# Two routing tables of a mixture-of-experts kernel, made from kept 16-bit one-hots in a row of products instead of one 32-bit one-hot at a time

## The chip, the cores and the metric

The kernel runs on one core of a Trainium2 chip. The metric is the device time of one execution in microseconds (us). Three runs of the kernel before gave 2086.29, 2083.27 and 2085.58 us, so a median of 2085.58.

## The reference

A network of two layers works on 1024 tokens of width 1024. Each layer has a mixer (a gated convolution in layer 0, sliding-window attention in layer 1), a normalisation, a mixture of 32 experts, and a second normalisation. The experts, cut to what matters here:

```python
g_idx = argmax(g_logits)                       # one of 4 groups a token
top_p, top_i = top_k(softmax(e_sel), 2)        # two of the group's 8 experts
gates = g_p * top_p / sum(top_p)               # a gate for each (token, choice)
# the rows that chose an expert are put in blocks of 128 rows; a block runs through
# its expert, and each row of the result is scaled by its gate and added to its token
ys = (silu(x @ wg[e]) * (x @ wu[e])) @ wd[e]
out = segment_sum(ys * row_gate[:, None], row_tok)
```

An expert that more than 128 tokens chose needs further blocks, the overflow. All of it is in 32 bits.

## The kernel before, in words

Products are made on the tensor engine (PE) in three parts: each 32-bit operand is split into a high and a low part, and `mm3` issues high by high, high by low and low by high. Weights come in chunks of 1 MB from SyncE's DMA queue into rings of buffers. ScalarE (ACT) makes a chunk's high part (`h`, L164), VectorE (DVE) its low part (`l`, L165), and then the raw buffer is free for a later chunk. The kernel's instructions keep the written order on each engine (`manual_schedule`, L50).

`proj_route` (L398) routes the tokens, 128 at a time. `place` (L514) finds for a token and a choice its place in its expert's list (`pos`) and makes a one-hot of that place over 128 slots, in 16 bits (`oh`, L522), in a tile of two buffers that is dropped after `tabulate` (L526) has used it for the table of token numbers.

`experts` (L718) then goes through the 32 experts, one block of 128 rows each. For expert e the order on PE is: half of the gate product `pg`, the other half, half of the up product `pu`, the transposes of the next block's rows (`xpose`, L731), the other half of `pu`, then the down product of expert e-1 (`pd`), and the transposes of the hidden values (`hid_pose`, L767). Chunks are split three ahead. After each of the first three halves of an expert, `extra` (L777) takes one step of a generator that makes what the routing still lacks: the softmax gates (`gates`, L601), the table of gates by slot and expert (`slot_gates`, L625), which `y_out` first needs at the third expert, and the overflow's tables (`overflow`, L643), which are needed after the last expert. So there are three steps an expert, and they are spread over the first 13 experts.

`slot_gates` makes, for each of the 16 pairs of a token block and a choice, a 32-bit one-hot of the place (`goh`, L636) and a row of the gate at the chosen expert (`ga`, L637), both on GpSimd (POOL), and adds their 32-bit product on PE into one PSUM tile (`pgate`, L630). `overflow` makes for each pair a 32-bit one-hot (`ooh`, L694) and two rows (`orr`, L696) on VectorE, one pair a step, and PE adds their product to `pov` (L698) at the next step.

Two more places matter. `xsplit` (L738) puts the split rows of a block in the tiles xh and xl, but those of the first block in the slots `yt0` and `yt1`, in which `y_out` (L762) puts the experts' results from the third expert on; each slot has one buffer. A tile that takes over a slot is written only when the last reader of the tile before it is done.

Of the kernel before, what the change touches and what calls it, by code (L numbers as in the profile page):

```python
# [11 lines left out]
F32 = mybir.dt.float32  # L12
F32R = mybir.dt.float32r
F16 = mybir.dt.float16
I32 = mybir.dt.int32
AF = mybir.ActivationFunctionType
OP = mybir.AluOpType
AX = mybir.AxisListType

P = 128  # L20
D = 1024
T = 1024
NB = T // P
NE = 32
EG = 8
NG = 4
DE = 512
NOV = 16
ALPHA = 4 ** 0.25
# [6 lines left out]
def moe_net_kernel(ctx, tc, a, dbg=None):  # L36
# [15 lines left out]
    # ---------------------------------------------------------------- weights  # L52
    # a chunk is 1 MB; each partition reads one contiguous run of 8 KB, so that tile s of a chunk of n
    # tiles holds its rows n * p + s
# [42 lines left out]
    # The raw chunks lie in rings of two: two rings always, except that heads of q take the second during  # L97
    # the attention, a third from the output projection to the experts' last, and four chunks in the room of
    # the mixer's output, from when it has been read to the experts' last.
# [17 lines left out]
    def pump(eng=nc.sync):  # L117
        while st["load"] < min(len(chunks), st["limit"]):
            i = st["load"]
            r = rings[i]  # L120
            if st["free"][r] == 0:
                return
            st["free"][r] -= 1
            st["load"] += 1
            if r == "rawy":
                raws[i] = st["ry"][st["rawy"] % 4].rearrange("p k f -> p (k f)")
                st["rawy"] += 1
            else:
                p = st[r] if r in ("rawb", "rawx") else rawp
                raws[i] = p.tile([P, 2048], F32, name=f"raw{i}", tag=r, bufs=2)  # L130
            src = chunks[i][0]
            if i == 1:
                # the first two chunks come in alternate quarters, that the work may start
                for q in range(4):
                    for j in range(2):
                        x = chunks[j][0].rearrange("p k f -> p (k f)")[:, q * 512:(q + 1) * 512]
                        nc.sync.dma_start(raws[j][:, q * 512:(q + 1) * 512], x)
            elif i > 1:
                eng.dma_start(raws[i].rearrange("p (k f) -> p k f", k=src.shape[1]), src)
# [6 lines left out]
    # 32 KB in two halves: the mixers' output, chunks, the norm's rows, heads of q  # L146
# [49 lines left out]
    def warm(n, ps, tag, bufs):  # L196
        # products for nothing where the tensor engine waits, that its clock stays up
        t = ps.tile([P, 512], F32, name=f"warm{n}", tag=tag, bufs=bufs)
        for _ in range(n):
            nc.tensor.matmul(t.rearrange("p (k f) -> p k f", k=4), ones16,  # L200
                             ones16[:, None, :].to_broadcast([P, 4, P]), start=True, stop=True)
# [8 lines left out]
    # -------------------------------------------------------------- constants  # L210
# [54 lines left out]
    # ------------------------------------------------- bias rows of attention  # L265
# [3 lines left out]
    def bias_rows(w, ps):  # L269
        tab = w.tile([32, 16], F32, name="tab")  # L270
        nc.gpsimd.dma_start(tab, a["rel_table"])
        oh = w.tile([32, 384], F32, name="oh")
        nc.gpsimd.dma_start(oh, a["buckets"])
        far = w.tile([16, 384], F32, name="far")
        nc.gpsimd.memset(far, -BIG)
        yield
        pb = ps.tile([16, 384], F32, name="pb", tag="mm", bufs=8)
        nc.tensor.matmul(pb, tab, oh, start=True, stop=True)
        nc.vector.tensor_copy(far[:, P:2 * P], pb[:, P:2 * P])
        nc.gpsimd.dma_start(bias_v, far)  # L280
        # row q lies q further right, so that a plain rectangle of it holds the relative positions
        nc.gpsimd.dma_start(bass.AP(tensor=bias_s.tensor, offset=bias_s.offset, ap=[[8193, P], [512, 16], [1, 384]]),
                            bass.AP(tensor=bias_v.tensor, offset=bias_v.offset, ap=[[0, P], [384, 16], [1, 384]]))

    # ------------------------------------------------------------ layer 0: A
    def mixer_in(y):
        with ExitStack() as s:
# [19 lines left out]
            # v, tokens on partitions  # L307
# [26 lines left out]
            # u, channels on partitions  # L334
# [15 lines left out]
            # spatial mixing of v and y_a  # L350
# [12 lines left out]
            # gated convolution  # L363
# [33 lines left out]
    # ------------------------- B: projection, residual, norm, routing, tables  # L397
    def proj_route(l, y, c0, resid, bias, x1d, acc, R, xgs):  # L398
        s = R["stack"]
        with ExitStack() as s2:  # L400
# [113 lines left out]
            def place(n):  # L514
                t = w.tile([P, NE], F32, name=f"q{n}", tag="rq", bufs=2)
                oh = w.tile([P, 2, P], F16, name=f"oh{n}", tag="oh", bufs=2)
# [19 lines left out]
            if bias is not None:  # L536
                # the residual is scaled by ALPHA after its bias
                nc.vector.tensor_scalar(bias, bias, 1.0 / ALPHA, None, op0=OP.mult)
# [61 lines left out]
    # ------------------------------------------ gates and overflow bookkeeping  # L600
    def gates(w, R):  # L601
        lg, em, mx = R["lg"], R["em"], R["mx"]
        ge = w.tile([P, NB, NG], F32, name="ge")
# [8 lines left out]
        s = w.tile([P, NB, 4], F32, name="gs")  # L612
# [8 lines left out]
        # the sum that they enter is the residual's, over ALPHA  # L621
        nc.vector.scalar_tensor_tensor(s[:, :, 3:4], s[:, :, 2:3], 1.0 / ALPHA, s[:, :, 0:1], op0=OP.mult, op1=OP.mult)
        nc.vector.tensor_tensor(R["gate"], pr, s[:, :, 3:4].to_broadcast([P, NB, 2]), op=OP.mult)

    def slot_gates(w, ps, R):  # L625
        pt = ps.tile([P, 512], F32, name="pgate", tag="misc", bufs=1)
        made, used = [], 0
        for make, use in ((4, 0), (2, 0), (4, 4), (6, 6), (0, 0), (0, 6)):
            for i in range(used, used + use):
                nc.tensor.matmul(pt[:, 0:NE], *made[i], start=(i == 0), stop=(i == 15))  # L630
            used += use
            for i in range(len(made), len(made) + make):
                n, j = i // 2, i % 2
                oh = w.tile([P, P], F32, name=f"goh{i}", tag="goh", bufs=6)
                ag = w.tile([P, NE], F32, name=f"ga{i}", tag="ga", bufs=6)
                nc.gpsimd.tensor_scalar(oh, slots, R["pos"][:, n, j:j + 1], None, op0=OP.is_equal)  # L636
                nc.gpsimd.tensor_scalar(ag, R["A"][:, n, j], R["gate"][:, n, j:j + 1], None, op0=OP.mult)  # L637
                made.append((oh, ag))
            if used < 16:
                yield  # L640
        nc.vector.tensor_copy(R["sgate"], pt[:, 0:NE])

    def overflow(w, ps, R):  # L643
# [6 lines left out]
        ov = w.tile([P, NE], F32, name="ov")  # L650
# [14 lines left out]
        ovs = w.tile([P, NE], F32, name="ovs")  # L665
# [22 lines left out]
        nc.vector.scalar_tensor_tensor(slot, q, -float(P), pos, op0=OP.mult, op1=OP.add)  # L688
        po = ps.tile([P, 512], F32, name="pov", tag="misc", bufs=1)
        gate = R["gate"].rearrange("p n j -> p (n j)")  # L690
        for i in range(16):
            oh = w.tile([P, P], F32, name=f"ooh{i}", tag="goh", bufs=6)
            rr = w.tile([P, 2, 16], F32, name=f"orr{i}", tag="ga", bufs=6)
            nc.vector.tensor_scalar(oh, slots, slot[:, i:i + 1], None, op0=OP.is_equal)  # L694
            for j, x in enumerate((rowm[:, i // 2:i // 2 + 1], gate[:, i:i + 1])):
                nc.vector.tensor_scalar(rr[:, j], slots[:, 0:16], oid[:, i:i + 1], x, op0=OP.is_equal, op1=OP.mult)  # L696
            yield
            nc.tensor.matmul(po[:, 0:32], oh, rr.rearrange("p j b -> p (j b)"), start=(i == 0), stop=(i == 15))  # L698
        nc.vector.tensor_scalar(R["ovidx"], po[:, 0:16], float(T), None, op0=OP.add)
        nc.vector.tensor_copy(R["ovgate"], po[:, 16:32])  # L700
# [16 lines left out]
    # ------------------------------------------------------------ the experts  # L717
    def experts(l, c0, x1d, acc, R, xg, consts, scratch):  # L718
        with ExitStack() as s:
# [4 lines left out]
            # the block after the last expert's is the first of those for the rows beyond an expert's 128  # L724
# [13 lines left out]
            def xsplit(e):  # L738
                # the first block's lie where the results will, that the second's need not wait
# [251 lines left out]
    # ---------------------------------------------- norm of residual and experts  # L991
    class Norm2:
        # the parts of the norm of residual and experts, block by block
# [64 lines left out]
        def beside(self, block, fix, more, gate):  # L1058
            # the rows of the block are done again with what it adds
# [30 lines left out]
    # ------------------------------------------------------------ attention  # L1090
    def attention(qs, kh, kl, v):
        with ExitStack() as s:
# [10 lines left out]
            # a unit's four heads lie even ones first  # L1103
# [92 lines left out]
    # ================================================================ program  # L1196
    def routing_state(p, l):
# [6 lines left out]
            "idx": p.tile([P, NE], I32, name=f"idx{l}"), "sgate": p.tile([P, NE], F32, name=f"sgate{l}"),  # L1204
            "meta": p.tile([P, 17], I32, name=f"meta{l}"), "ovidx": p.tile([P, 16], I32, name=f"ovidx{l}"),
# [41 lines left out]
    with ExitStack() as s0:  # L1247
        kvp = pool("kv", st=s0)
        # a head's q, and k, each lie as the high part above the low one
# [157 lines left out]
def layout(inputs):  # L1407
# [9 lines left out]
    # channel tiles u, then (gate c, h, gate b) per tile, two tiles a chunk  # L1417
# [33 lines left out]
```

## Time and profile before

| what | value |
|---|---|
| median of 3 runs | 2085.58 us (2083.27 to 2086.29) |
| profiled execution, its span | 2086.2 us |
| PE busy | 1931.8 us (93%) |
| PE weight load busy | 1565.7 us (75%) |
| VectorE busy | 1580.8 us (76%) |
| ScalarE busy | 1206.1 us (58%) |
| GpSimd busy | 476.9 us (23%) |
| weight DMA queue (q1) | 487.41 MB, 61.6% of 16 engines' span |

The page gives no time of the profiled execution beside its span; the span lies 0.1 us under the slowest of the three runs, so that nothing to be seen lies around it. Busy time is the union of an engine's instructions. Matmuls are pipelined and their ends are modelled, so starts are the surer reading. A wait is named by what released it.

### The profile page before, as it was taken

To read this page: it belongs to the slowest core of one execution; us is meant where nothing else is said; L and a number is where in the kernel's file an instruction comes from. 1 tells how busy PE (TensorE), PEld (TensorE's weight loads), DVE (VectorE), ACT (ScalarE), POOL (GpSimd) and SP (SyncE) were. 2 spreads that over 40 slices of the span, in tenths; PEclk is the share of its full clock that TensorE was granted. 3 is DMA by queue.
4 is the path that set the end of the run, shared out by engine and by line. 5 is a ranking of instruction groups with operands and counts; after the bars stand their busy time and mean duration, and the time that the engine had idled before them with its cause. 6 is when DMAs were issued, how large, how long until landed. Compare 5 with 4: busy or idle time off the path is not lost. (4 is left out here: it accounts for less than half of the span.)

```text
span 2086.2 us, 24852 instructions
## 1 busy us (share of the span) xinstructions
PE 1931.8 (93%) x9264; PEld 1565.7 (75%) x9264; DVE 1580.8 (76%) x2020; ACT 1206.1 (58%) x1246; POOL 476.9 (23%) x319
## 2 busy tenths in 40 slices
PE   8999998899999999998598989979999999999990
PEld 7888786687778888887487767757877888888870
DVE  3533587599888888887643996976898888888876
ACT  4211211477677777776454872125777777777763
POOL 0100003622111211212300552146121112112116
PEclk9999998899999999999799999989999999999995
DMA  6141536599969999997511006366999699999983
GB/s 249 41 122 41 192 112 242 192 335 371 345 228 363 371 364 377 369 371 281 225 41 62 21 21 232 125 248 219 374 357 355 218 379 360 368 376 364 380 282 145
DMA packets 97215, 527.59 MB, mean 253 GB/s; under 512 B 19668, under 2 KB 21732, under 8 KB 43840
## 3 DMA queue, kind: packets, MB, share of 16 engines
q1 hardware_dynamic: 76992, 487.41, 61.6%
q0 software_dynamic: 20096, 38.52, 7.4%
q8 instruction: 75, 1.23, 0.2%
q14 instruction: 52, 0.43, 0.1%
HBM read 501.58 MB, written 62.94 MB: 271 GB/s over the span
## 5 line engine op out<-in xcount | busy, mean ns | idle before, releaser
L165 DVE TENSOR_TENSOR l<-raw,h 128x2048 fp32r<-128x2048 f32 (+2 forms) x356 | 797.4, 2261 | 108.3 <-ACT h L164 104.0
L164 ACT CAST h<-raw 128x2048 fp32r<-128x2048 f32 (+1 forms) x363 | 678.2, 1884 | 130.9 <-PE pu L206 38.0
L713 POOL DMA_INDIRECT acc<-y,idx x64 | 127.5, 1993 | 605.7 <-ACT y L764 578.9
L204 PE MATMUL pu<-h,xh 128*128 128x512 f32 x512 | 209.5, 409 | 0.0
L204 PE MATMUL pg<-h,xh 128*128 128x512 f32 x512 | 208.6, 407 | 0.0
L204 PE MATMUL pd<-h,hh 128*128 128x512 f32 x512 | 203.2, 397 | 1.4 <-ACT hh L164 1.4
L206 PE MATMUL pg<-h,xl 128*128 128x512 f32 x512 | 203.0, 397 | 1.0 <-DVE xl L165 1.0
L206 PE MATMUL pu<-h,xl 128*128 128x512 f32 x512 | 203.1, 397 | 0.0
L205 PE MATMUL pu<-l,xh 128*128 128x512 f32 x512 | 202.9, 396 | 0.0
L206 PE MATMUL pd<-h,hl 128*128 128x512 f32 x512 | 202.0, 395 | 0.0
L205 PE MATMUL pg<-l,xh 128*128 128x512 f32 x512 | 201.7, 394 | 0.0
L205 PE MATMUL pd<-l,hh 128*128 128x512 f32 x512 | 201.4, 393 | 0.0
L703 POOL DMA_INDIRECT xg<-x1d,idx x64 | 96.6, 1510 | 354.0 <-PE pt L735 340.2
L164 ACT CAST xh<-pt 128x1024 fp32r<-128x1024 f32 x66 | 67.0, 1016 | 126.5 <-PE pu L205 110.2
L848 DVE TENSOR_TENSOR sg<-sg,pu 128x512 f32<-128x512 f32 x64 | 44.0, 687 | 110.8 <-PE pu L206 110.8
L206 PEld LDWEIGHTS pg<-h,xl 128*128 128x128 f32 x512 | 96.0, 188 | 25.2 <-DVE xl L165 1.9
L206 PEld LDWEIGHTS pd<-h,hl 128*128 128x128 f32 x512 | 96.0, 187 | 24.9 <-DVE hl L165 0.9
L206 PEld LDWEIGHTS pu<-h,xl 128*128 128x128 f32 x512 | 96.6, 189 | 23.7
L165 DVE TENSOR_TENSOR l<-ry,h 128x2048 fp32r<-128x2048 f32 x48 | 109.9, 2296 | 5.9 <-ACT h L164 5.9
L204 PEld LDWEIGHTS pd<-h,hh 128*128 128x128 f32 x512 | 96.0, 187 | 24.4 <-ACT hh L164 1.7
L205 PEld LDWEIGHTS pd<-l,hh 128*128 128x128 f32 x512 | 96.0, 187 | 23.1
L204 PEld LDWEIGHTS pu<-h,xh 128*128 128x128 f32 x512 | 97.6, 191 | 20.1
(326 smaller groups left out, 3844.8 us busy)
## 6 DMA issues: line engine op xcount, KB each, us to landing
raw<-in_w_gate SPq DMA_DIRECT2D x128, 1024.0 KB, 8.3
raw<-in_w_up SPq DMA_DIRECT2D x104, 1024.0 KB, 10.5
raw<-in_w_down SPq DMA_DIRECT2D x104, 1024.0 KB, 10.6
ry<-in_w_up SPq DMA_DIRECT2D x24, 1024.0 KB, 8.1
ry<-in_w_down SPq DMA_DIRECT2D x24, 1024.0 KB, 10.0
raw<-in_w_in SPq DMA_DIRECT2D x8, 1024.0 KB, 6.4
x1d<-xr SPq DMA_DIRECT2D x16, 512.0 KB, 2.7
acc<-xr SPq DMA_DIRECT2D x16, 512.0 KB, 3.9
```

What stands on the lines that cost most here:

```text
L164: (high or nc.scalar.copy)(h, x)
L165: (eng or nc.vector).tensor_tensor(l, x, h.bitcast(F32), op=OP.subtract)
L204: nc.tensor.matmul(out, sh, mh, start=start, stop=False)
L205: nc.tensor.matmul(out, sh, ml, start=False, stop=False)
L206: nc.tensor.matmul(out, sl, mh, start=False, stop=stop)
L703: nc.gpsimd.indirect_dma_start(out=rows, out_offset=None, in_=src, in_offset=bass.IndirectOffsetOnAxis(ap=idx, axis=0), bounds_check=T - 1 ...
L713: nc.gpsimd.indirect_dma_start(out=acc, out_offset=bass.IndirectOffsetOnAxis(ap=idx, axis=0), in_=rows, in_offset=None, bounds_check=T - 1 ...
L848: nc.vector.tensor_tensor(sg, sg, pu, op=OP.mult)
```

## The change

The 16-bit one-hots of `place` now go to a tile of the routing state, `R["oh"]`, of 16 by 128 values a partition, and stay there. `slot_gates` no longer makes one-hots: it splits the gates in three 16-bit parts whose sum is the gate, multiplies all 16 rows of choices by each part in one VectorE instruction, and then issues 16 products of 16 bits in a row, each with 96 columns (three parts of 32 experts); the three parts are added from PSUM. `overflow` makes its rows for all 16 pairs at once, remakes the one-hots in place, four pairs to an instruction, and then also issues 16 products in a row. Some small tiles share slots to make room. The comments were taken out, which left the line numbers of most of the kernel as they were.

```diff
-                oh = w.tile([P, 2, P], F16, name=f"oh{n}", tag="oh", bufs=2)
+                oh = R["oh"][:, 2 * n:2 * n + 2]
...
+    PARTS = (1.0, 2.0 ** -11, 2.0 ** -22)
+
+    def gate_parts(w, R):
+        gp = R["gp"] = w.tile([P, 3, 16], F16, name="gp")
+        rest = w.tile([P, 16], F32, name="gr")
+        x = R["gate"].rearrange("p n j -> p (n j)")
+        for c in range(3):
+            nc.vector.tensor_scalar(gp[:, c], x, 1.0 / PARTS[c], None, op0=OP.mult)
+            if c < 2:
+                nc.vector.scalar_tensor_tensor(rest, gp[:, c], -PARTS[c], x, op0=OP.mult, op1=OP.add)
+                x = rest
+
+    def add_parts(out, parts):
+        nc.vector.tensor_copy(out, parts[0])
+        for c in (1, 2):
+            nc.vector.scalar_tensor_tensor(out, parts[c], PARTS[c], out, op0=OP.mult, op1=OP.add)
+
     def slot_gates(w, ps, R):
+        gate_parts(w, R)
+        yield
+        A = R["A"].rearrange("p n j e -> p (n j) e")
+        ag = w.tile([P, 16, 3, NE], F16, name="ag", tag="yt1", bufs=1)
+        for c in range(3):
+            nc.vector.tensor_tensor(ag[:, :, c], A, R["gp"][:, c, :, None].to_broadcast([P, 16, NE]), op=OP.mult)
+            if c > 0:
+                yield
         pt = ps.tile([P, 512], F32, name="pgate", tag="misc", bufs=1)
-        made, used = [], 0
-        for make, use in ((4, 0), (2, 0), (4, 4), (6, 6), (0, 0), (0, 6)):
-            for i in range(used, used + use):
-                nc.tensor.matmul(pt[:, 0:NE], *made[i], start=(i == 0), stop=(i == 15))
-            used += use
-            for i in range(len(made), len(made) + make):
-                n, j = i // 2, i % 2
-                oh = w.tile([P, P], F32, name=f"goh{i}", tag="goh", bufs=6)
-                ag = w.tile([P, NE], F32, name=f"ga{i}", tag="ga", bufs=6)
-                nc.gpsimd.tensor_scalar(oh, slots, R["pos"][:, n, j:j + 1], None, op0=OP.is_equal)
-                nc.gpsimd.tensor_scalar(ag, R["A"][:, n, j], R["gate"][:, n, j:j + 1], None, op0=OP.mult)
-                made.append((oh, ag))
-            if used < 16:
-                yield
-        nc.vector.tensor_copy(R["sgate"], pt[:, 0:NE])
+        for i in range(16):
+            nc.tensor.matmul(pt[:, 0:3 * NE], R["oh"][:, i], ag[:, i].rearrange("p c e -> p (c e)"),
+                             start=(i == 0), stop=(i == 15))
+        add_parts(R["sgate"], [pt[:, c * NE:(c + 1) * NE] for c in range(3)])
+        yield
...
         slot = w.tile([P, 16], F32, name="slot")
         nc.vector.scalar_tensor_tensor(slot, q, -float(P), pos, op0=OP.mult, op1=OP.add)
+        rr = w.tile([P, 16, 4, 16], F16, name="orr", tag="cmp", bufs=1)
+        sel = rr[:, :, 0]
+        nc.vector.tensor_tensor(sel, slots[:, None, 0:16].to_broadcast([P, 16, 16]),
+                                oid[:, :, None].to_broadcast([P, 16, 16]), op=OP.is_equal)
+        yield
+        for c in range(3):
+            nc.vector.tensor_tensor(rr[:, :, c + 1], sel, R["gp"][:, c, :, None].to_broadcast([P, 16, 16]), op=OP.mult)
+            yield
+        sel = sel.rearrange("p (n j) b -> p n j b", j=2)
+        nc.vector.tensor_tensor(sel, sel, rowm[:, :, None, None].to_broadcast([P, NB, 2, 16]), op=OP.mult)
+        yield
+        for i in range(0, 16, 4):
+            nc.vector.tensor_tensor(R["oh"][:, i:i + 4], slots[:, None, :].to_broadcast([P, 4, P]),
+                                    slot[:, i:i + 4, None].to_broadcast([P, 4, P]), op=OP.is_equal)
+            yield
         po = ps.tile([P, 512], F32, name="pov", tag="misc", bufs=1)
-        gate = R["gate"].rearrange("p n j -> p (n j)")
         for i in range(16):
-            oh = w.tile([P, P], F32, name=f"ooh{i}", tag="goh", bufs=6)
-            rr = w.tile([P, 2, 16], F32, name=f"orr{i}", tag="ga", bufs=6)
-            nc.vector.tensor_scalar(oh, slots, slot[:, i:i + 1], None, op0=OP.is_equal)
-            for j, x in enumerate((rowm[:, i // 2:i // 2 + 1], gate[:, i:i + 1])):
-                nc.vector.tensor_scalar(rr[:, j], slots[:, 0:16], oid[:, i:i + 1], x, op0=OP.is_equal, op1=OP.mult)
-            yield
-            nc.tensor.matmul(po[:, 0:32], oh, rr.rearrange("p j b -> p (j b)"), start=(i == 0), stop=(i == 15))
+            nc.tensor.matmul(po[:, 0:64], R["oh"][:, i], rr[:, i].rearrange("p c b -> p (c b)"),
+                             start=(i == 0), stop=(i == 15))
+        yield
         nc.vector.tensor_scalar(R["ovidx"], po[:, 0:16], float(T), None, op0=OP.add)
-        nc.vector.tensor_copy(R["ovgate"], po[:, 16:32])
+        add_parts(R["ovgate"], [po[:, 16 + 16 * c:32 + 16 * c] for c in range(3)])
...
+            "oh": p.tile([P, 16, P], F16, name=f"oh{l}"),
```

## Rows read from the trace of the kernel before

**Rows 1.** Two windows: length, busy PE, PEld, DVE, ACT, POOL, PE clock, DMA share, GB/s.
```profile
703.00:722.00 19.00, 19.00 (x89) 15.54 (x89) 16.60 (x10) 15.01 (x11) 3.60 (x2) 1.00 1.00 389
...
412.00:413.00 1.00, 1.00 (x6) 0.90 (x5) 0.00 (x0) 0.00 (x0) 0.00 (x0) 0.50 0.00 0
```

**Rows 2.** Timeline of ACT: start, duration, instruction; one silu an expert.
```profile
500.63 0.60 ACT L833 ACTIVATE sg<-pg 128x512 f32<-128x512 f32 x1 [0.41 <-PE pg L206]
...
620.53 0.60 ACT L833 ACTIVATE sg<-pg 128x512 f32<-128x512 f32 x1 [0.64 <-PE pg L206]
...
693.44 0.60 ACT L833 ACTIVATE sg<-pg 128x512 f32<-128x512 f32 x1 [0.41 <-PE pg L206]
...
711.67 0.60 ACT L833 ACTIVATE sg<-pg 128x512 f32<-128x512 f32 x1 [0.41 <-PE pg L206]
...
1527.81 0.60 ACT L833 ACTIVATE sg<-pg 128x512 f32<-128x512 f32 x1 [0.41 <-PE pg L206]
...
1646.16 0.60 ACT L833 ACTIVATE sg<-pg 128x512 f32<-128x512 f32 x1 [0.63 <-PE pg L206]
```

**Rows 3.** Who waited for whom: SyncE's DMA queue, the whole span.
```profile
SPq L139 <- DVE l L165: 1227.4, 344, 27.3
...
SPq L242 <- DVE y L388: 17.3, 1, 17.3
```

**Rows 4.** Timeline of PE, layer 0, first two experts; in brackets the idle time before.
```profile
388.90 0.97 PE L630 MATMUL pgate<-ga,goh 128*128 128x32 f32 x8
389.71 1.18 PE L735 MATMUL pt<-ident,xg 128*128 128x128 f32 x8
390.65 0.48 PE L204 MATMUL pu<-h,xh 128*128 128x512 f32 x1
...
393.28 0.39 PE L206 MATMUL pu<-h,xl 128*128 128x512 f32 x1
...
396.77 1.42 PE L630 MATMUL pgate<-ga,goh 128*128 128x32 f32 x12
398.03 0.49 PE L204 MATMUL pg<-h,xh 128*128 128x512 f32 x1
...
403.72 0.30 PE L630 MATMUL pgate<-ga,goh 128*128 128x32 f32 x2
406.65 0.64 PE L630 MATMUL pgate<-ga,goh 128*128 128x32 f32 x2 [2.63 <-POOL ga L637]
...
410.79 1.95 PE L735 MATMUL pt<-ident,xg 128*128 128x128 f32 x8
412.38 0.78 PE L204 MATMUL pu<-h,xh 128*128 128x512 f32 x1
...
413.64 0.39 PE L204 MATMUL pu<-h,xh 128*128 128x512 f32 x1
```

**Rows 5.** Timeline of PE, layer 1, second expert.
```profile
1430.69 0.30 PE L630 MATMUL pgate<-ga,goh 128*128 128x32 f32 x2
...
1437.77 1.95 PE L735 MATMUL pt<-ident,xg 128*128 128x128 f32 x8
```

**Rows 6.** Timeline of DVE, layer 0, first expert.
```profile
389.15 2.29 DVE L165 TENSOR_TENSOR l<-raw,h 128x2048 fp32r<-128x2048 f32 x1 [1.42 <-ACT h L164]
391.98 1.22 DVE L165 TENSOR_TENSOR xl<-pt,xh 128x1024 fp32r<-128x1024 f32 x1 [0.53 <-ACT xh L164]
393.71 0.69 DVE L848 TENSOR_TENSOR sg<-sg,pu 128x512 f32<-128x512 f32 x1 [0.51 <-PE pu L206]
```

**Rows 7.** Tile cmp: forms, duration in ns (least, median, most), first and last start.
```profile
L668 DVE TENSOR_TENSOR cmp<-inc,slots x2: 681/681/681, 487.3 to 1514.5; 128x512 f32<-128x512 f32 x2
```

**Rows 8.** Timeline of PE in proj_route, layer 0: two 16-bit products in a stream.
```profile
275.74 0.21 PE L529 MATMUL pidx<-ri,oh 128*128 128x32 f16 x2
275.81 0.47 PE L204 MATMUL pm<-h,yx 128*128 128x512 f32 x1
```

**Rows 9.** Timeline of PE, layer 0, tenth expert.
```profile
561.89 0.41 PE L698 MATMUL pov<-orr,ooh 128*128 128x32 f32 x2 [0.57 <-DVE orr L696]
```

More of the change, by code (lines that the diff above doesn't have):

```diff
@@ L602, in gates @@
         lg, em, mx = R["lg"], R["em"], R["mx"]
-        ge = w.tile([P, NB, NG], F32, name="ge")
+        ge = w.tile([P, NB * NG], F32, name="ge", tag="inc", bufs=2).rearrange("p (n g) -> p n g", n=NB)
         nc.vector.tensor_tensor(ge, lg[:, :, 0:NG], mx[:, :, 0:1].to_broadcast([P, NB, NG]), op=OP.subtract)
@@ L611, in gates @@
         yield
-        s = w.tile([P, NB, 4], F32, name="gs")
+        s = w.tile([P, NB * 4], F32, name="gs", tag="ov", bufs=1).rearrange("p (n g) -> p n g", n=NB)
         nc.vector.tensor_reduce(s[:, :, 0:1], ge, axis=AX.X, op=OP.add)
@@ L649, in overflow @@
         nc.vector.tensor_copy(cnt, pc[:, 0:NE])
-        ov = w.tile([P, NE], F32, name="ov")
+        ov = w.tile([P, NE], F32, name="ov", tag="ov", bufs=1)
         q = w.tile([P, 16], F32, name="q")
@@ L664, in overflow @@
             yield
-        ovs = w.tile([P, NE], F32, name="ovs")
+        ovs = w.tile([P, NE], F32, name="ovs", tag="inc", bufs=2)
         nc.vector.tensor_tensor(ovs, inc, ov, op=OP.subtract)
```

## The prediction

> **What bounds the kernel now.** I began with the page: PE is busy for 93% of the span, and its chain of waits covers only the last five microseconds, so it says nothing about the experts. So I went to windows. In a stretch of the experts past the tables PE is busy for all 19.00 of 19 us at full clock, VectorE for 16.60, and the DMA engines all the time [rows 1]. Is PE the bound there, or the transfers? Two views decide. The silu of ACT falls once an expert, and its distance is 711.67 - 693.44 = 18.23 us [rows 2], the same over the experts around it, as steady as only a queue that waits for nothing can be. And SyncE, which issues the weight loads, waited 1227.4 us in 344 waits for VectorE to free a raw buffer [rows 3]: the loads are held back by the consumers, not the reverse; in the microsecond from 412 the DMA engines even stand still [rows 1]. So each microsecond that PE loses in the experts is a microsecond of the span, and the change is priced on PE's timeline.
>
> There the two tables stand out. Both are steps of the generator, thus inside PE's stream, and PE keeps its order: where a table's operand is late, the experts' products behind it are late too.
>
> **What is removed.** *The gate table, layer 0* [rows 4]. The first four products (8 instructions) put xpose off by 389.71 - 388.90 = 0.81 us, the next six (12 instructions) the gate product by 398.03 - 396.77 = 1.26. The last six begin at 403.72, and xpose, which follows, starts at 410.79: 7.07 us, of which 2.63 before one product alone, since POOL is still making goh and ga. After it the clock is low (0.50, that is 1.2 GHz, in the window from 412 [rows 1]): xpose takes 412.38 - 410.79 = 1.59 where it took 390.65 - 389.71 = 0.94, and the next three products 413.64 - 412.38 = 1.26 where products start 0.24 apart ((393.28 - 390.65)/11), thus 0.72 to 0.78. That is 0.65 + 0.5 more. Sum: 10.3. In layer 1 the same stop is 1437.77 - 1430.69 = 7.08 [rows 5], so I take 10.3 again.
>
> *The overflow's table* [rows 2]. From the silu of expert 6 to that of expert 12 it is 620.53 - 500.63 = 119.90 us in layer 0 and 1646.16 - 1527.81 = 118.35 in layer 1, against 6 x 18.23 = 109.38 undisturbed: 10.5 and 9.0. It is 16 pairs of 32-bit products and PE's waits for orr, such as 0.57 [rows 9].
>
> Together 10.3 + 10.3 + 10.5 + 9.0 = 40.1 us. POOL's own work on goh and ga lies beside PE but for that stop; its gathers come earlier, which nobody waits for.
>
> **What is added.** *The gate table.* gate_parts is five small VectorE instructions right after the gates, while VectorE waits for ACT's next chunk: nothing (at most 0.5 if that cover were gone, since the chunk is needed an expert later). Then comes the step on which I stake most. The table ag goes to slot yt1, and there the low half of the first block's rows still lies (xsplit, first expert). The generator's second step makes ag, in the middle of that expert, but the last reader of the old tile is the last product of its pu. So VectorE's first ag instruction waits for that product, and VectorE keeps its order: behind it stand the other part of ag, the low part of chunk 5, the third part, and then xl of the second block, without which PE can't go on into expert 1.
>
> I follow it in layer 0. Without the 0.81 us of the old products the last product of pu ends at 393.28 + 0.39 - 0.81 = 392.86 [rows 4]. An ag part has 128 x 512 elements and a broadcast operand, as L668 with 0.68 us [rows 7]; it starts the next about 0.6 later. So: two parts to 394.1, chunk 5 (2.29 busy, the next starts after 2.2 [rows 6]) to 396.3, the third part to 396.9, xl (1.22) to 398.1. PE has started the second product of expert 1 by then and would start the third, the first that reads xl, at about 393.1. It stops for 5.0 us. Before, xl was done at 393.2 and nothing waited. From below: if the wait for the slot doesn't arise, 0; if a part takes half of 0.68, 4.0. From above: if each takes double, 7.0. I take 5.0, as L668 has the same size and an equal kind of operand. A stop of 4.6 us and more without a product is longer than the one of 2.63 after which the clock was low, so I add the low-clock loss of then, 1.1 (0 to 1.4).
>
> The 16 products in a row: in the stream of proj_route two 16-bit products took 0.07 us until the next started [rows 8], thus 0.035 each; the 32-bit instructions took 0.81/8 = 0.10 each [rows 4]. So 0.6 to 1.6 us for 16; I take 1.0. They come late in expert 1's first half, when ag is long done. add_parts (three small VectorE instructions) falls where VectorE waits for ACT; y_out, the reader, is an expert away.
>
> Once PE goes on, nothing else is late: chunk 6 follows xl and sg on VectorE (0.6 and 2.3 us, done by 401), and PE wants it after two halves of 12 products, the table's 16 and the low clock's loss, at about 398.1 + 5.8 + 1.0 + 1.1 = 406.
>
> One rule of the Trainium skill prices the products higher ("TensorE: Matmul & The Clock Gate", Back-to-back issue gap): a steady stream of weight loads and products of 128 columns is given as about 81 ns a product. By it 16 take 1.3 us, an estimate, and the four tables 1.2 us more than I say; by the pair of rows 8 they would take 1.8 us less. No row of this trace has so many in a stream.
>
> *The overflow's table.* Nine VectorE instructions of 256 or 512 elements an overflow replace 48 small ones, one step each, inside VectorE's slack (18.23 less some 15.9 an expert, from 16.60 in 19 us [rows 1]). The 16 products come in the second step of expert 9 and need the last quarter of the one-hots, which VectorE makes in the first step, behind the low part of a chunk. That is the position of the old wait of 0.57 [rows 9]; PE now comes some 0.2 to 0.25 earlier (no product in the first step), and 0.68 stands for three instructions of 0.6 in all. So it waits 0.9 (0 to 2), and the products take 1.0.
>
> *The one-hots that are kept* cost no instruction. The state grows by 4 KB a partition and the pools behind it move up. What they wait for is the stage before, as l1g shows, which waits 17.3 us for that stage's last VectorE instruction [rows 3]; that can't get later. Nothing, then.
>
> **Sum.** Added per layer 5.0 + 1.1 + 1.0 + 0.9 + 1.0 = 9.0, twice 18.0. Net 40.1 - 18.0 = 22.1 us less. The profiled execution had a span of 2086.2 us, 0.6 over the median of the runs, so 2064.1 on its own time and 2063.5 on the median. With the ends of the added terms (park 4 to 7 and clock 0 to 1.4, products 0.6 to 1.6, the last wait 0 to 2) it is 2057 to 2071, more likely 2058.5 to 2068.5, as not all go one way.
>
> **Rivals.** *No park* (chance 0.13). If ag's first write doesn't wait for pu, the 6.1 us per layer fall away: 2063.5 - 12.2 = 2051.3. For it: VectorE is idle for 1.42 us before chunk 5's low part [rows 6], and two parts fit in there. Against it: the slot has one buffer and a reader yet to come.
>
> *More stops* (0.13). VectorE comes out of the park and through experts 6 to 8 late, PE waits longer at expert 9, and its clock falls there as well: 2 + 1.4 more a layer, about 2070. For it: a VectorE with 2.3 us of slack an expert. Against it: VectorE's work in the overflow gets less.
>
> *The loads take over* (0.06). If PE's pace ran into the transfers, whose engines show no idle time in rows 1, PE would wait for weights as long as it saves: 2083 to 2086, no change. Against it: SyncE's waits for buffers, and a DMA that stands still in the stop that goes.
>
> *VectorE becomes the bound, and the kernel is slower* (0.04). The place is experts 6 to 9 and ag; the price is that of a 512-element instruction on broadcast 16-bit values. Three ag parts lie whole in PE's stop, and nine instructions of the overflow share four experts' slack of 2.3 us, 9 in all, and a start of about 3 from the chunks split ahead. At x us each the added cost is 3(x - 0.68) + max(0, 9x - 12) beyond my sum; at x = 2.1 it is 4.3 + 6.9 = 11.2 a layer, and the gain of 11 is spent. At 3 us each: 7.0 + 15.0 = 22 a layer, 2063.5 + 44 = 2107. Against it: L668 with 0.68.
>
> **How the numbers follow.** Forecast 0.64, the rivals 0.13, 0.13, 0.06 and 0.04. The likeliest gives 2063.5. The range goes from the rival without the park to the one with more stops, 2050 to 2071; outside it are both tails and the last two rivals, 0.18. A measurement of this kernel can tell 0.2%, 4.2 us, from no change; faster by more are the first three cases, 0.90, no change 0.06, slower 0.04.
>
> **What would show it.** Right: after the change VectorE's first ag instruction waits for PE's pu of expert 0 in both layers, PE then idles about 5 us before the third product of expert 1 on xl, at a clock that falls to half afterwards; no POOL instruction but the gathers there; silu 0 to silu 2 some 38 us (two experts' 36.5, less 5.8 for the 24 down products that expert 0 hasn't before it, and 7.1 for the stop, the clock and the table); silu 6 to silu 12 some 111.3, with one wait of about 0.9 in expert 9. Wrong: silu 1 coming within 14 us of silu 0 (no park), a silu distance above 18.3 in other experts (VectorE or the loads), or a time above 2071.

## The result, and the profile after

The changed kernel took 2060.35 us as the median of four runs (2054.84 to 2063.94), the kernel before 2085.77 in four runs (2083.27 to 2086.29): a ratio of 0.987, 95% interval 0.985 to 0.989, some 25 us less. The profile is that of the run of 2054.84, span 2053.2. In five more rounds (below) the two medians were 2061.61 and 2088.73, ratio 0.987 (0.985 to 0.989).

First the page: busy time by engine, and the one group of TensorE's products that waited for xl (after the bar: idle time before the group, then what ended it).

```profile
PE 1902.9 (93%) x9200; PEld 1551.4 (76%) x9200; DVE 1575.9 (77%) x1966; ACT 1206.0 (59%) x1246; POOL 436.5 (21%) x255
...
L206 PE MATMUL pg<-h,xl 128*128 128x512 f32 x512 | 204.6, 400 | 10.8 <-DVE xl L165 10.8
```

The step on which the prediction staked most is there. VectorE in layer 0, first expert (start, duration, instruction, in brackets its idle time and what ended it), which answers to [rows 6]:

```profile
392.47 1.29 DVE L649 TENSOR_TENSOR ag<-A,gp 128x512 f16<-128x512 f32 x2 [5.03 <-PE pu L206]
393.68 2.29 DVE L165 TENSOR_TENSOR l<-raw,h 128x2048 fp32r<-128x2048 f32 x1
395.88 0.69 DVE L649 TENSOR_TENSOR ag<-A,gp 128x512 f16<-128x512 f32 x1
396.48 1.22 DVE L165 TENSOR_TENSOR xl<-pt,xh 128x1024 fp32r<-128x1024 f32 x1
```

and the tile ag over both layers:

```profile
L649 DVE TENSOR_TENSOR ag<-A,gp x6: 684/685/694, 392.5 to 1404.7; 128x512 f16<-128x512 f32 x6
its engine sat idle before it (us, times) until:
  PE pu L206: 10.1, 2
```

So ag waits in both layers until the last product of pu has read the tile that lay in its slot, 5.03 us, and the chunk's low part and xl stand behind it. What that does to TensorE, and the overflow's products in expert 9, which answers to [rows 4] and [rows 9]:

```profile
392.27 0.39 PE L204 MATMUL pg<-h,xh 128*128 128x512 f32 x1
392.50 0.40 PE L205 MATMUL pg<-l,xh 128*128 128x512 f32 x1
397.76 0.80 PE L206 MATMUL pg<-h,xl 128*128 128x512 f32 x1 [4.86 <-DVE xl L165]
398.35 0.63 PE L204 MATMUL pg<-h,xh 128*128 128x512 f32 x1
...
401.77 0.63 PE L206 MATMUL pg<-h,xl 128*128 128x512 f32 x1
402.19 0.87 PE L798 MATMUL ph<-ident,sg 128*128 128x128 f32 x4
402.90 0.84 PE L654 MATMUL pgate<-ag,oh 128*128 128x96 f16 x16
403.56 0.48 PE L204 MATMUL pg<-h,xh 128*128 128x512 f32 x1
...
551.44 0.52 PE L723 MATMUL pov<-orr,oh 128*128 128x64 f16 x12
552.51 0.29 PE L723 MATMUL pov<-orr,oh 128*128 128x64 f16 x4 [0.55 <-DVE oh L718]
552.63 0.48 PE L204 MATMUL pu<-h,xh 128*128 128x512 f32 x1
```

Read the starts: 4.86 us without a product, then products 0.43 apart where they stood 0.23 apart. The windows (length; busy PE, PEld, DVE, ACT, POOL; PE clock; DMA share; GB/s) show why, and the last of them answers to [rows 1]:

```profile
392.50:397.80 5.30, 0.44 (x3) 0.04 (x1) 5.30 (x6) 0.01 (x1) 0.00 (x0) 0.82 0.23 65
397.80:402.20 4.40, 4.40 (x11) 3.33 (x12) 2.70 (x2) 0.00 (x0) 0.00 (x0) 0.50 0.63 240
402.20:407.30 5.10, 5.10 (x37) 4.45 (x36) 2.47 (x2) 4.20 (x4) 0.00 (x0) 0.95 0.42 173
...
691.00:710.00 19.00, 19.00 (x91) 15.81 (x90) 16.65 (x10) 14.25 (x10) 3.55 (x2) 1.00 1.01 381
```

The granted clock is at half, 1.2 GHz, for the 4.4 us behind the stop; in layer 1, where the stop is 4.86 us too, seven products run slowly and not ten. The Trainium skill ("TensorE: Matmul & The Clock Gate", Part 1) gives 426.7 ns from product to product of 512 columns at the low clock; the rows agree, 0.427 on average from 398.35 to 401.77.

Last the silus of experts 0, 2, 6, 12, 16, 17 and 18, which answer to [rows 2]:

```profile
386.43 0.60 ACT L860 ACTIVATE sg<-pg 128x512 f32<-128x512 f32 x1
...
424.89 0.60 ACT L860 ACTIVATE sg<-pg 128x512 f32<-128x512 f32 x1 [0.43 <-PE pg L206]
...
497.35 0.60 ACT L860 ACTIVATE sg<-pg 128x512 f32<-128x512 f32 x1 [0.42 <-PE pg L206]
...
607.30 0.60 ACT L860 ACTIVATE sg<-pg 128x512 f32<-128x512 f32 x1 [0.42 <-PE pg L206]
...
679.75 0.60 ACT L860 ACTIVATE sg<-pg 128x512 f32<-128x512 f32 x1 [0.42 <-PE pg L206]
...
697.81 0.60 ACT L860 ACTIVATE sg<-pg 128x512 f32<-128x512 f32 x1 [0.29 <-PE pg L206]
...
715.98 0.60 ACT L860 ACTIVATE sg<-pg 128x512 f32<-128x512 f32 x1 [0.42 <-PE pg L206]
```

From these: 38.46 us from silu 0 to silu 2 (41.03 before; in layer 1 37.60 for 41.19), 109.95 from 6 to 12 (119.90 before). And one thing that no step had: far from both tables the silus stand 18.06 and 18.17 us apart in turn, not 18.23. It shows all through both layers' experts, but for expert 9 and the last four of layer 1.

### The profile page after: what moved, and what is told of

Read it like the earlier page. It is cut to its first block, busy times and chain, and to the rows that moved or that the text cites. A ratio compares the mean times of both kernels' runs of the same rounds, so it can differ in the third digit from the quotient of the medians.

```text
span 2053.2 us, 24597 instructions
## 1 busy us (share of the span) xinstructions
PE 1902.9 (93%) x9200; PEld 1551.4 (76%) x9200; DVE 1575.9 (77%) x1966; ACT 1206.0 (59%) x1246; POOL 436.5 (21%) x255
## 5 line engine op out<-in xcount | busy, mean ns | idle before, releaser
L730 POOL DMA_INDIRECT xg<-x1d,idx x64 | 107.5, 1680 | 386.7 <-PE pt L762 362.8
L204 PEld LDWEIGHTS pg<-h,xh 128*128 128x128 f32 x512 | 97.9, 191 | 20.3 <-issue 0.6
L205 PEld LDWEIGHTS pg<-l,xh 128*128 128x128 f32 x512 | 97.3, 190 | 20.4
```

The source lines that it names most:

```text
L204: nc.tensor.matmul(out, sh, mh, start=start, stop=False)
L205: nc.tensor.matmul(out, sh, ml, start=False, stop=False)
L730: nc.gpsimd.indirect_dma_start(out=rows, out_offset=None, in_=src, in_offset=bass.IndirectOffsetOnAxis(ap=idx, axis=0), bounds_check=T - 1 ...
```

## The experiments

Runs with the same median of before were taken together, on one chip, beside it. "Room" is ag in dead room, "late" the overflow's products a step later.

| run | edit | median us | before | ratio (95%) |
|---|---|---|---|---|
| e1_again | none | 2061.61 | 2088.73 | 0.987 (0.985 to 0.989) |
| e2_own_room | room | 2046.24 | 2088.73 | 0.980 (0.978 to 0.981) |
| e3_warm | work in the stop | 2056.85 | 2088.73 | 0.985 (0.983 to 0.988) |
| e4_room_late | room, late | 2045.74 | 2088.73 | 0.979 (0.978 to 0.981) |
| e5_before_32 | the kernel before, moved by 32 bytes | 2082.23 | 2087.03 | 0.997 (0.996 to 0.999) |
| e6_after_aligned | hlb moved by 32 bytes | 2058.28 | 2087.03 | 0.986 (0.985 to 0.988) |
| e7_after_x32 | xh to hl moved by 32 bytes | 2066.54 | 2087.03 | 0.991 (0.989 to 0.992) |
| e8_best | room, late, hlb moved | 2041.46 | 2087.03 | 0.978 (0.977 to 0.980) |
| e9_hlb256 | e8, all 128 bytes down | 2049.15 | 2088.20 | 0.982 (0.980 to 0.983) |
| e10_x128 | e8, xh to hl 64 bytes up | 2041.71 | 2088.20 | 0.977 (0.976 to 0.979) |
| e11_both | e9, xh to hl 64 bytes up | 2047.18 | 2088.20 | 0.980 (0.978 to 0.981) |

**The park, taken away.** Theory: the stop comes from the slot that ag shares with the first block's low part. The rivals: the loads follow no faster, or the clock falls anyway.

```diff
-        ag = w.tile([P, 16, 3, NE], F16, name="ag", tag="yt1", bufs=1)
+        ag = w.tile([P, 10, 3, NE], F16, name="ag", tag="cmp", bufs=1)
+        ah = R["lg"].rearrange("p n g -> p (n g)").bitcast(F16).rearrange("p (i c e) -> p i c e", c=3, e=NE)
...
+            row = ag[:, i] if i < 10 else ah[:, i - 10]
```

> The changed kernel, with ag not in the room of the first block's low part (yt1) but in dead room: ten of its sixteen rows in the tag of cmp, six over the logits, which nothing reads any more. VectorE makes six products for three, same elements. Theory A (the prediction's step 'park', with the clock's loss behind it): the 5.03 us wait of VectorE's first ag goes, PE has no stop of 4.86 us before the third product of expert 1 and no stretch at half clock, and the Silus of experts 0 and 2 stand about 31 to 32 us apart in place of 38.46 (0.7 us for the sixteen products at most). That is 7 us a layer, 14 in all: median about 2046. Rival B (the loads take over): the weight loads cannot follow faster, the time comes back as waits for loads by expert 6, and the median stays within 3 us of the changed kernel's, 2057 to 2063. Rival C (the clock falls for another reason than the stop): only the 5 us a layer go, median about 2050.

Measured: 2046.24, which is 15.4 under the changed kernel in the same comparison. Silu 0 to silu 2 takes 31.44 us in both layers. TensorE at the same place, and its clock:

```profile
393.51 0.40 PE L205 MATMUL pg<-l,xh 128*128 128x512 f32 x1
394.02 0.50 PE L206 MATMUL pg<-h,xl 128*128 128x512 f32 x1
394.36 0.40 PE L204 MATMUL pg<-h,xh 128*128 128x512 f32 x1
...
396.90 0.59 PE L658 MATMUL pgate<-ag,oh 128*128 128x96 f16 x10
397.32 0.42 PE L658 MATMUL pgate<-lg,oh 128*128 128x96 f16 x6
397.56 0.48 PE L204 MATMUL pg<-h,xh 128*128 128x512 f32 x1
```

```profile
392.50:397.80 5.30, 5.19 (x38) 4.16 (x37) 4.34 (x6) 1.73 (x3) 0.52 (x1) 1.00 0.74 257
```

The product that stopped for 4.86 us comes 0.51 behind the one ahead of it, and the clock stays at 1.00. Both rivals fall. The sixteen products take 397.56 - 396.90 = 0.66 us at full clock.

**The clock, apart from the stop.** Here TensorE works for nothing while it waits:

```diff
+                    if e == 1:
+                        warm(18, ps, "misc", 1)
                     gu(e, 0, c, pg)
```

> The changed kernel, with 18 products for nothing (128x512, results unused) ahead of expert 1's first, so that TensorE works for about 4.1 of the 4.9 us for which it waits for xl. The stop itself stays. Theory A: the stop costs its own 4.86 us and then some 2.4 us more, because the granted clock behind it is half for about 5 us; with TensorE at work the clock stays at full and these 2.4 us a layer go: expert 0's Silu to expert 2's 36 us for 38.46, median 4 to 5 us under the changed kernel's. Rival B: the half clock isn't the stop's doing, or the products cost what they save: median within 1.5 us of the changed kernel's.

```profile
393.22 4.06 PE L200 MATMUL warm<-ones 128*128 128x512 f16 x18
...
397.35 0.40 PE L205 MATMUL pg<-l,xh 128*128 128x512 f32 x1
398.70 0.50 PE L206 MATMUL pg<-h,xl 128*128 128x512 f32 x1 [0.96 <-DVE xl L165]
399.04 0.39 PE L204 MATMUL pg<-h,xh 128*128 128x512 f32 x1
```

The product on xl comes as long after pu as in the changed kernel, and the next ones are 0.23 apart. The windows of the wait and of what follows it have the clock at full:

```profile
393.00:398.60 5.60, 4.74 (x22) 2.06 (x20) 5.19 (x6) 0.46 (x1) 0.00 (x0) 1.00 0.22 65
398.60:402.00 3.40, 3.30 (x24) 2.86 (x25) 2.84 (x3) 0.21 (x1) 0.00 (x0) 1.00 0.64 267
```

Silu 0 to 2 takes 36.21 in both layers, where the changed kernel has 38.46 and 37.60 in its first trace and 38.54 and 38.11 in e1_again: the clock's share is 2.2 to 2.3 us in layer 0 and 1.4 to 1.9 in layer 1. The other 4.77 (36.21 - 31.44) is the stop itself. The median is 4.8 us lower, about what the theory said.

**The overflow's wait.**

```diff
+        yield
         po = ps.tile([P, 512], F32, name="pov", tag="misc", bufs=1)
```

> The kernel with ag in dead room, and the sixteen overflow products one step later (one third of an expert), so that the four large VectorE operations that remake oh are done before them. Theory A: the wait of 0.55 us a layer before the first of these products goes, 1.1 us in all against the kernel with ag in dead room: about 2045. Rival B: another product of TensorE waits for VectorE in its place, since the four operations of 0.68 us delay the split behind them wherever the products stand: no change, about 2046.

The medians, 2045.74 and 2046.24, can't tell 1.1 us. The traces can: no product for pov waits, and silu 9 to silu 10 takes 18.83 for 19.44 in both layers. The theory holds, at 0.61 us a layer.

**The shorter period: the run's or the kernel's?**

> The changed kernel again, nothing edited. Its first trace differs from the trace before in one thing that no step of the prediction has: in the experts' steady stretch the time from one Silu to the next is 18.06 and 18.17 us in turn (mean 18.115), where it was 18.22, because part of the 128x512 products start 226 ns apart. Over some 55 such periods that is 6 us. Theory A: the spacing belongs to the kernel (where its tiles lie, or how its instructions stand), so this trace shows 18.06 and 18.17 again, and the median stays near 2060. Rival B: it belongs to the single execution; then this trace may show 18.22, and the times spread over some 9 us again, the higher ones with the longer period.

18.06 and 18.17 again in both layers, as in the three runs above: it is the kernel's. The spread of the times is not its doing, since the two traces of the changed kernel have the same period and belong to runs of 2054.84 and 2061.09. Most of that difference lies outside the experts: from the silu of layer 0's last expert to that of layer 1's first it takes 443.87 us in the first trace and 449.52 in the second. Why that stretch varies stays open.

What differs far from the tables is where the tiles lie. The kept one-hots push all later pools 4096 bytes up, and the tiles that went and came shift xh, xl, hh and hl, the split rows and hidden values that are the products' stationary operands, by 544. I took the starts of the products in a trace and averaged their distances over each chunk of twelve. With the split chunk in the pair of buffers hla: 233 ns before, 229 after; in hlb: 233 before, 234 after. The places of xh, xl, hh and hl, at 32 bytes over a multiple of 64 before and at a multiple of 64 after, suggested a rule: products start closer where both operands lie at multiples of 64 bytes. Three runs tried it.

```diff
-        gp = R["gp"] = w.tile([P, 3, 16], F16, name="gp")
+        gp = R["gp"] = w.tile([P, 4, 16], F16, name="gp")[:, 0:3]
-        rest = w.tile([P, 16], F32, name="gr")
+        rest = w.tile([P, NE], F32, name="gr", tag="ov", bufs=1)[:, 0:16]
```

> The changed kernel with xh, xl, hh and hl 32 bytes off a multiple of 64, as in the kernel before (gp 32 bytes longer, gr moved into another's room), and hlb where the changed kernel has it. Theory A: the hla products go back to 233 ns, the Silus to 18.22 us apart, and the median rises by some 6.5 us, to about 2068; that is the part of the gain that no step of the prediction had. Rival B: the period stays 18.115 and the median about 2061.

Silus 6, 12, 16, 17 and 18:

```profile
498.11 0.60 ACT L860 ACTIVATE sg<-pg 128x512 f32<-128x512 f32 x1 [0.41 <-PE pg L206]
...
608.63 0.60 ACT L860 ACTIVATE sg<-pg 128x512 f32<-128x512 f32 x1 [0.41 <-PE pg L206]
...
681.52 0.60 ACT L860 ACTIVATE sg<-pg 128x512 f32<-128x512 f32 x1 [0.41 <-PE pg L206]
...
699.75 0.60 ACT L860 ACTIVATE sg<-pg 128x512 f32<-128x512 f32 x1 [0.40 <-PE pg L206]
...
717.97 0.60 ACT L860 ACTIVATE sg<-pg 128x512 f32<-128x512 f32 x1 [0.41 <-PE pg L206]
```

18.23 and 18.22: the period of before is back, the hla products are at 233 ns, and the median is 5 to 6 us above the changed kernel's in the two other comparisons (7 by the ratios). So 32 bytes in the place of the stationary parts are worth about that, and this run shows the change without it: 20.5 us less than before (interval 16.5 to 22.7).

The other way round, the kernel before with every later tile 32 bytes up, and the changed one with hlb moved:

```diff
-            "idx": p.tile([P, NE], I32, name=f"idx{l}"), "sgate": p.tile([P, NE], F32, name=f"sgate{l}"),
+            "idx": p.tile([P, NE], I32, name=f"idx{l}"), "sgate": p.tile([P, NE + 8], F32, name=f"sgate{l}")[:, 0:NE],
```

> The kernel before, with one tile of the routing state 32 bytes longer (sgate has 8 columns more, unused), so that every tile behind it lies 32 bytes further in SBUF; nothing else. In the changed kernel's steady stretch the products whose moving operand is a split chunk of the one pair of buffers (hla) start 228.6 to 229.9 ns apart, those of the other pair (hlb) 233.8 to 234.5; in the kernel before both start 232.6 to 234.2 apart. hla stands at a multiple of 64 bytes in both kernels, hlb at 32 over one in both; the stationary parts xh, xl, hh and hl stand at 32 over one in the kernel before and at a multiple of 64 in the changed one. Theory A: 128x512 products are faster where both operands stand at multiples of 64 bytes. Here all of them do: 229 ns each, the Silus 17.9 us apart in place of 18.22, and some 62 such periods make the kernel about 19 us faster than before (ratio 0.991). Rival B: what counts is something else of the change (the 4096 bytes by which hlb moved, or the place of the instructions): ratio 1.000.

> The changed kernel with hlb at a multiple of 64 bytes too: sgate 32 bytes longer, gp 32 bytes longer to keep xh, xl, hh and hl where they are, and the small tile gr moved into another's room to make place. Theory A (both operands at multiples of 64 bytes): the hlb products, 36 of an expert's 72, also start 229 ns apart, the Silus 17.92 us apart in place of 18.115, and the median falls by some 12 us, to about 2050. Rival B: no change, about 2061.

The second has the lines of both diffs above; its median is 2058.28, its period 18.05 and 18.14. It differs from e7_after_x32 by the sgate line alone and was taken in the same comparison: 32 bytes make 8.3 us between them, and 62 periods of 0.13 are 8.1.

Silus 16 to 18 of the kernel before so moved:

```profile
692.13 0.60 ACT L833 ACTIVATE sg<-pg 128x512 f32<-128x512 f32 x1 [0.40 <-PE pg L206]
...
710.18 0.60 ACT L833 ACTIVATE sg<-pg 128x512 f32<-128x512 f32 x1 [0.30 <-PE pg L206]
...
728.32 0.60 ACT L833 ACTIVATE sg<-pg 128x512 f32<-128x512 f32 x1 [0.41 <-PE pg L206]
```

18.05 and 18.14: nothing but 32 bytes, and the kernel before is 0.26% faster (0.15 to 0.36). But I had expected 19 us and got 5, since only the hla products got faster; hlb's stayed at 233 in both kernels, at a multiple of 64 bytes as well. That half of the rule is wrong. By the period alone it would be 8 us; in this trace TensorE's waits in the two tables and for late low parts in layer 1's last experts are 2.6 us longer than in the trace of before.

> The kernel with ag in dead room and the overflow products a step later, and all operands at multiples of 64 bytes. If the causes add: 2045.7 less 12, about 2034, ratio 0.974 of before. If the loads set the pace once the products are faster (they are at 0.98 to 1.0 of the DMA engines' time in the steady stretch now): the period stays above 18.0 us, TensorE waits for splits of late chunks, and the median stays above 2040.

2041.46, period 18.05 and 18.14: the causes add but for hlb's. It is 4.3 us under e4_room_late, but in another comparison; the ratios, 0.978 and 0.979, differ by 2 us, 62 periods of 0.02 are 1.2, and neither is clear of the noise. No product of the steady stretch waited for a late chunk.

Three more places asked whether hlb's products have a place of their own. Small tiles of the overflow's bookkeeping went over em, which is dead by then, to make room (in e9_hlb256 the overflow's row numbers and gates as well, first pair of lines, which takes 128 bytes from the routing state; in e10_x128 gp grows, second pair; e11_both has the two).

```diff
-            "meta": p.tile([P, 17], I32, name=f"meta{l}"), "ovidx": p.tile([P, 16], I32, name=f"ovidx{l}"),
+            "meta": p.tile([P, 17], I32, name=f"meta{l}"), "ovidx": dead[:, NE + 64:NE + 80].bitcast(I32),
...
-        gp = R["gp"] = w.tile([P, 4, 16], F16, name="gp")[:, 0:3]
+        gp = R["gp"] = w.tile([P, 6, 16], F16, name="gp")[:, 0:3]
```

> The kernel with ag in dead room, the overflow products a step later and the operands at multiples of 64 bytes, with hlb at a multiple of 256 bytes, as hla is (128 over one so far): some small tiles of the overflow's bookkeeping lie over em, which nothing reads by then. Shown so far: a move of the stationary parts by 32 bytes takes the hla products from 233 to 229 ns; a move of hlb by 32 bytes leaves its products at 233. Open: why hlb's stay there. Theory A: the moving operand has to stand at a multiple of 256 bytes; then the hlb products go to 229 ns, the Silus stand 17.92 us apart in place of 18.093, and the time falls by some 10 us, from 2041.5 to 2031. Rival B: it is hlb's place in SBUF or who writes there meanwhile, no matter at which multiple: 18.09 us and 2041.

> The same base, with xh, xl, hh and hl at multiples of 128 bytes (64 over one so far), hlb as it was (128 over a multiple of 256). Theory A: the stationary parts are what the hlb products still wait for, and a place 64 bytes on changes them as a place 32 bytes on changed those of hla: 17.92 us from Silu to Silu and 2031. Rival B: at 64 bytes nothing more is to be had: 18.09 us and 2041.

> Both moves: hlb at a multiple of 256 bytes, xh, xl, hh and hl at multiples of 128. Theory A (only with both operands there are all 128x512 products fast): 17.92 us from Silu to Silu, 2031. Rival B: 18.09 us and 2041, so that hlb's products are slower for a reason that no place tried here touches.

The periods: 18.22, 18.03 and 18.17. With hlb at a multiple of 256 and xh at one of 64 bytes, all products are at 233 again, so the rule of 64 falls altogether; with xh 64 bytes up, the hla products reach 227 in some chunks, and those of hlb stay at 231 to 234. So the place decides, by up to 0.2 us an expert, but I found no rule for which place is good, and no run tells the mechanism: that stays open.

Through all this the loads come closer. ScalarE's waits for a gate chunk, whole span, changed kernel and e10_x128 (engine, line, waited for: us, times, longest):

```profile
ACT h L164 <- DMA raw<-in_w_gate: 11.8, 12, 2.1
```

```profile
ACT h L164 <- DMA raw<-in_w_gate: 23.6, 18, 2.2
```

In the kernel before they were 8.6 us in 9 waits. In layer 1's last experts this shows: the changed kernel's silus stand 18.44, 18.53 and 18.34 us apart there, up to 19.04 in e10_x128, since ScalarE makes a late chunk's high part first. TensorE's transposes still start 18.12 and 18.11 us apart there (18.04 and 18.11 in e10_x128), so up to there it loses nothing. Its last down products, though, wait 1.2 us for hh and 0.8 for hl in e10_x128, where the changed kernel has 0.7 for hh alone; hh stands on ScalarE behind the high part of the last down chunk, for which ScalarE waited 2.76 us. So at 18.0 us an expert little is left.

## Why the prediction was right, point by point

The time was 3 us under the forecast, and the mechanism is the one that was forecast. That it came so near is in part luck: errors inside the sum cancel, and a gain that wasn't in it, 6 to 7 us, took the time from 3 us above the forecast (2066.54 in e7_after_x32) to 3 us below.

- *The gate table's removal, 10.3 a layer.* Held. Silu 0 to 2 was 41.03 and 41.19 us before; with ag in dead room it is 31.44, of which 0.66 are new products, and 0.2 is the shorter period. The old table's part is 10.0 and 10.2.
- *The park, 5.0.* Held: 4.86 in the trace, 4.77 between e3_warm and e2_own_room. An ag part took 0.685 us for the 0.68 that I took from another line, and the order behind it on VectorE is the forecast one.
- *The clock, 1.1.* Mis-sized: 1.4 to 2.3, at and above the end of 1.4 that I gave. I took the loss behind the stop of before, where the clock had already been low inside the stop, with products trickling through, and only eight transposes and three products ran slowly after it:

```profile
408.00:409.00 1.00, 0.72 (x3) 0.58 (x3) 0.00 (x0) 0.00 (x0) 1.00 (x3) 0.50 1.04 344
```

Here seven to ten products ran at half, and in layer 0 the transposes.
- *The sixteen products, 1.0 and 1.0.* Too dear: 0.66 for the gate's (41 ns each) and 552.63 - 551.44 - 0.55 = 0.64 for the overflow's. The nearest row, the pair at 35 ns, was the better guide. The Trainium skill ("TensorE: Matmul & The Clock Gate", Back-to-back issue gap) gives 81 ns for products of 128 columns, which I gave beside it; that is twice what these streams of 96 and 64 columns took.
- *The wait at expert 9, 0.9.* 0.55 in the trace, 0.61 by e4_room_late. Here the step had the overlap wrong. VectorE began the last quarter of oh 0.33 us after TensorE came to the products:

```profile
551.77 0.68 DVE L718 TENSOR_TENSOR oh<-slots,slot 128x512 f16<-128x512 f32 x1
```

TensorE came to the products at 551.44 and to the last four at 552.51, 1.07 later, so that quarter was no earlier than I had it. But only four of the sixteen products read it; the other twelve ran in the meantime. I had added the wait and the products as if one followed the other.
- *The overflow's table.* Forecast 111.3 us from silu 6 to 12; e7_after_x32, at the period of before, has 110.52 in both layers, for 119.90 and 118.35 without the change. The difference to the forecast is the cheaper products and wait.
- *The sum.* Added in layer 0: 4.86 + 2.25 + 0.66 + 0.55 + 0.64 = 8.96, in layer 1, with a clock of 1.39, 8.1, where I had 9.0 twice. In e7_after_x32 the change is worth 20.5 (16.5 to 22.7), where I had 22.1.
- *The one-hots that are kept: "Nothing, then."* The step that failed. Their instructions cost nothing, but "the pools behind it move up" was not nothing: with the tiles that went, it moved the stationary parts, and that is 0.11 us in each of some 60 periods, 6 to 7 us.

Of the rivals, *no park* had its price nearly right: the kernel that really has none is 15.4 us faster than the changed one by the medians, 13.2 by the silus of the first traces (7.02 and 6.16), for 12.2 by my sum, which had the clock too cheap; its silu 1 comes 13.75 us after silu 0, under the 14 that I had named, and the changed kernel's 20.77. *More stops* and *VectorE* didn't come: from expert 2 on the silus stand never more than 18.17 us apart but at expert 9, until the last experts of layer 1. There they are above the 18.3 that I had named as a sign of being wrong, but TensorE's products aren't late for it: it is ScalarE that waits for loads. *The loads take over* is what later gains will meet.

The best kernels here, e8_best and e10_x128, are the same within what can be measured, 0.978 (0.977 to 0.980) of the kernel before.

## What to carry to other kernels

When a new tile takes a slot of one buffer, ask who reads the old tile last in the order of the program, and what stands behind the writer on its engine: here that was 6 to 7 us a layer, and dead room for the tile was at hand. Count the clock with a stop: work for nothing in the wait gave back a fifth to a third of what stop and clock cost. And when a change moves every later tile, compare the spacing of untouched instructions far from it before giving the edit the credit.

## What the runs showed of the hardware

- The place of tiles in SBUF changed how far apart 128x512 products started, from 227 to 234 ns, the same all through both layers' experts and, where a kernel was traced twice, in both traces; 32 bytes were enough (18.115 to 18.22 us an expert). The Trainium skill ("SBUF — State Buffer", Operand start alignment) asks of an operand's start that it be a multiple of the element's size. These runs do not contradict that, but they show that such places are not equally fast.
- After a stop of 4.86 us the clock was at half (0.50) for 4.4 us more in layer 0; with products for nothing in the stop it stayed at 1.00 (e3_warm).
- Sixteen 16-bit products of 96 columns, each with its own weights, took 41 ns each in a stream; sixteen of 64 columns took 40 ns each (0.64 us in all).
